# Changing over the two 64-token chunks of every second head pair in an RWKV recurrence

## The chip, the cores and the metric

The kernel runs on one core of a Trainium2 chip. The metric is the device time of one execution in microseconds, the median of several runs. All data are float32 in memory; the wide products are split into high and low float32r parts and take three passes each.

## The reference

One layer of a diffusion transformer: a feed-forward part, a mixer with two branches (retention and RWKV-7) in both directions over 1024 latent and 256 context tokens, and a second feed-forward part. The change concerns the RWKV branch, 8 heads of 64 in two directions:

```
def step(s, inp):                       # per token, per direction z and head
    rt, wt, kt, vt, at, bt = inp        # a = -kk, b = kk * a
    sa = einsum('zbhvk,zbhk->zbhv', s, at)
    s_new = s * wt[..., None, :] + sa[..., :, None] * bt[..., None, :] \
          + vt[..., :, None] * kt[..., None, :]
    y = where(is_fwd, einsum(s_new, rt), einsum(s, rt))
    return s_new, y
```

The output of both directions is added, normalised per head, scaled by `ln_w` and `ln_b`, a bonus term `sum(r * k * r_k) * v` is added, and the whole is multiplied by a gate.

## The kernel before

The stages follow each other: modulation vectors and the first feed-forward part (to about 1005 us of the trace), the projections of r, k, v and the low-rank decay terms (`rkv`, `lora_out`), then the recurrence, with the other projections of the mixer as filling work; then retention, the two output merges, the output projection and the second feed-forward part.

The 1280 tokens are cut into ten blocks of 128 (two of them context, p = 8 and 9), and each block into two chunks of 64. Both directions (z = 0 and 1) walk through the ten blocks, so there are 20 items, each of them for all 8 heads, kept as four head pairs `hp` with two heads `h` on the 128 partitions. For each item:

- `prep` (L738) loads the inputs, forms the decayed keys `bk` and queries `ar`, and multiplies them to the masked 128 x 128 matrices `g` (products `gps`, L793, copied by VectorE in L796). `ab(e)` gives the rows of chunk e: 64 to 127 for e = 0, 0 to 63 for e = 1.
- `inverse` (L828) inverts the 32 x 32 triangular blocks of `g` on VectorE, in 30 steps of two instructions (`invt` L846, `invx` L847), after a transfer through memory (`scr`, `invn`, L840) and a copy by ScalarE (L842) that spread the blocks over the partitions.
- `join` (L855) combines two 32-blocks to the inverse of 64: three sets of eight 32 x 32 products (`tps` L865, `hps` L868, `xps` L871) for e = 0, then the same for e = 1. Between the sets ScalarE copies (`tt`, L866 and L869), and VectorE writes the result back (L872). Each set has its own tile in PSUM, under the tag `us` with two buffers.
- `chain` (L874) is the recurrence: for each of the two chunks, the state products `q<-S,ar` (L888, four, 128 x 128 for latent blocks, which give the part for both halves of the partitions at once), the products of the chunk with v (`q<-wv,g`, L890, eight of 64 x 64), a copy `qa` (L892), the product with the inverse (`u<-qa,g`, L895, eight of 64 x 64), a copy to `wv` (L896), the state's addition (`u<-wv,bt`, L900, eight with 64 output rows, of which those of h = 0 and h = 1 lie in different halves), the state's decay on GpSimd (L902) and its sum on VectorE (L904), and for latent blocks the output products (`q<-wv,g`, L907, eight) and a copy or addition to `y` (L909, L911).
- `readout` normalises the finished blocks.

In one step all 24 products of L890, L895 and L907 have the same chunk e for all head pairs, so the same rows of the operands and the same rows of the output. There are 40 such steps, 32 of them with output.

`fill` runs beside it: `qkvg` and `gates` are 72 blocks of 24 wide products (`fps<-uh`, `fps<-ul`, L78 to L80, 512 or 256 columns), 1728 in all, whose weights are split by ScalarE (L67) and GpSimd (L68). The order of the instructions on each engine is not written out: a scheduler sets it from its own costs when the kernel is built, with the recurrence ahead of the fill by the order of the program.

The functions that the change touches, with what calls them:

Of the kernel before, what the change touches and what calls it, by code (L numbers as in the profile page):

```python
# [17 lines left out]
P = 128  # L18
# [377 lines left out]


class Mixer:
    def __init__(self, K, cst):
# [128 lines left out]
    def lora_out(self, c0, n, w2, pool, pk):  # L528
# [4 lines left out]
        def piece(q):  # L533
            if q == 0:
                st["x"] = pool.tile([96, 4, 512], F32R, tag="l2x", name="l2x", bufs=1)[:, :, :n]
                for b, s in enumerate("hlh"):
                    src = self.dram["wa" + s].rearrange("(q p) t -> p q t", p=32)[:, :, c0:c0 + n]
                    nc.sync.dma_start(out=st["x"][32 * b:32 * b + 32].bitcast(F32), in_=src)
            dst = self.dram[("td", "na")[q // 2] + str(q % 2)]
            for h0 in (0, 2):  # L540
                self.turns = self.turns[1:] + self.turns[:1]
                o = pool.tile([P, KT, P], F32, tag=self.turns[0], name="l2o", bufs=1).rearrange("p k c -> p (k c)").rearrange("p (h t) -> p h t", h=2)[:, :, :n]
                for j in range(2):
                    hp = h0 + j
                    ps = pk.tile([P, 512], F32, tag="l2", name="l2ps", bufs=2)[:, :n]
                    nc.tensor.matmul(ps, w2[:, q, hp * P:(hp + 1) * P], st["x"][:, q], start=True, stop=True)
                    nc.scalar.activation(o[:, j], ps, AF.Tanh, scale=0.5, bias=self.hw0[:, 4 * q + hp:4 * q + hp + 1])
                if q > 1:
                    nc.vector.tensor_scalar(out=o, in0=o, scalar1=-0.5, scalar2=-0.5, op0=ALU.mult, op1=ALU.add)
                nc.sync.dma_start(out=dst[h0:h0 + 2, :, c0:c0 + n].rearrange("h p t -> p h t"), in_=o)  # L550
        return [lambda q=q: piece(q) for q in range(4)]


    def rkv(self, u, pool, pp, pk):
# [8 lines left out]
        def heads(j, nm, hps):  # L563
# [14 lines left out]
            for hp, pad in zip(hps, pads):  # L578
                s = pool.tile([P, T], F32, tag="rs", name="rs", bufs=3)
                c = j * 4 + hp  # L580
                for t0, n in ((0, TL), (TL, TC))[:1 if j == 0 else 2]:
                    o = pcol(t0)
                    sv, pv = s[:, t0:t0 + n], pad[:, o:o + n]
                    nc.vector.tensor_tensor(out=sv, in0=pad[:, o - 1:o - 1 + n], in1=pad[:, o + 1:o + 1 + n], op=ALU.add)
                    nc.scalar.activation(pv, pv, AF.Copy, scale=om[:, c:c + 1])
                    nc.vector.scalar_tensor_tensor(out=sv, in0=sv, scalar=hm[:, c:c + 1], in1=pv, op0=ALU.mult, op1=ALU.add)
                    nc.sync.dma_start(out=self.dram[nm][hp, :, t0:t0 + n], in_=sv)
# [124 lines left out]
def ab(c):  # L712

    return 0 if c % 2 else 64

# [5 lines left out]
class Rwkv(Mixer):  # L721
# [16 lines left out]
    def prep(self, s, z, ring, tmp, pp):  # L738
# [62 lines left out]
        if z == 0 and lat:  # L801
# [4 lines left out]
            for hp in range(4):  # L806
                nc.tensor.matmul(ps[:, hp], self.cst["blk"], x[:, hp], start=True, stop=True)
            TT(out=x, in0=d["v"], in1=ps, op=ALU.mult)
            nc.sync.dma_start(out=self.dram["bv", p].rearrange("h p t -> p h t"), in_=x)
# [45 lines left out]
    def join(self, g, tmp, pq):  # L855

        nc, K = self.nc, self.K
        tt = tmp.tile([P, 8, 32], F32, tag="tt", name="tt")
        for e in range(2):
            of, os = ab(e), ab(e) + 32  # L860
            rf, rs = slice(of, of + 32), slice(os, os + 32)
            gb = lambda r, q, c: g[r, e, q // 2, q % 2, c]
            pst, psh, psx = (pq.tile([P, 8, 32], F32, tag="us", name=nm) for nm in ("tps", "hps", "xps"))
            for q in range(8):
                nc.tensor.matmul(pst[rf, q], gb(rf, q, rf), K.ident[rf, rf], start=True, stop=True, tile_position=(of, of))  # L865
            nc.scalar.activation(tt[rf], pst[rf], AF.Copy)  # L866
            for q in range(8):
                nc.tensor.matmul(psh[rs, q], gb(rf, q, rs), tt[rf, q], start=True, stop=True, tile_position=(of, os))  # L868
            nc.scalar.activation(tt[rs], psh[rs], AF.Copy)  # L869
            for q in range(8):  # L870
                nc.tensor.matmul(psx[rf, q], tt[rs, q], gb(rs, q, rs), start=True, stop=True, tile_position=(os, of))  # L871
            nc.vector.tensor_copy(out=g[rf, e, :, :, rs].rearrange("p a b t -> p (a b) t"), in_=psx[rf])  # L872

    def chain(self, un, z, y, first, last, tmp, ps_):  # L874
# [4 lines left out]
        hc = [slice(64 * h, 64 * h + 64) for h in range(2)]  # L879
        every = [(hp, h) for hp in range(4) for h in range(2)]  # L880
        lat, S = p < 8, self.S[z]
        f4 = lambda x: x.rearrange("p h v -> p (h v)")
        for e in (0, 1) if z == 0 else (1, 0):
            A, R = slice(ab(e), ab(e) + 64), slice(64 - ab(e), 128 - ab(e))
            q = ps_.tile([P, 4, P], F32, tag="q", name="q")
            qr, ac = (slice(0, P), slice(0, P)) if lat else (A, A)
            for hp in range(4):
                mm(q[qr, hp], ar[:, hp, e, ac], S[:, hp], start=hp == 0, stop=False)  # L888
            for hp, h in every:
                mm(q[A, hp, hc[h]], g[R, e, hp, h, A], wv[R, hp, e, hc[h]], start=False, stop=(hp, h) == (3, 1))  # L890
            qa = tmp.tile([P, 4, P], F32, tag="qa", name="qa")
            nc.scalar.activation(qa[A], q[A], AF.Copy)  # L892
            us = ps_.tile([P, 4, P], F32, tag="us", name="u")
            for hp, h in every:
                mm(us[A, hp, hc[h]], g[A, e, hp, h, A], qa[A, hp, hc[h]], start=True, stop=True)  # L895
            nc.scalar.activation(wv[A, :, e], us[A], AF.Copy)  # L896
            if not (last and e == 1 - z):
                st = us.rearrange("p h v -> p (h v)")[:, :256].rearrange("p (h v) -> p h v", h=4)
                for hp, h in every:
                    mm(st[hc[h], hp], bt[:, hp, e, hc[h]], wv[:, hp, e, hc[h]], start=True, stop=True)  # L900
                for h in range(2):
                    nc.gpsimd.tensor_tensor(out=S[hc[h], :, hc[h]], in0=S[hc[h], :, hc[h]], in1=pc[hc[h], e::2].unsqueeze(2).to_broadcast([64, 4, 64]), op=ALU.mult)  # L902
                for h in range(2):
                    nc.vector.tensor_tensor(out=S[hc[h], :, hc[h]], in0=S[hc[h], :, hc[h]], in1=st[hc[h]], op=ALU.add)  # L904
            if lat:
                for hp, h in every:
                    mm(q[R, hp, hc[h]], g[:, e, hp, h, R], wv[:, hp, e, hc[h]], start=False, stop=(hp, h) == (3, 1))  # L907
                if first:
                    nc.scalar.activation(y[R], f4(q[R]), AF.Copy)  # L909
                else:  # L910
                    nc.vector.tensor_tensor(out=y[R], in0=y[R], in1=f4(q[R]), op=ALU.add)  # L911
            yield

    def readout(self, p, y, tmp, pp):
# [20 lines left out]
        for hp in range(4):  # L935
            nc.vector.tensor_scalar(out=o[:, hp], in0=ps[:, hp], scalar1=K.vec["rwkv_ln_w"][:, hp:hp + 1], scalar2=K.vec["rwkv_ln_b"][:, hp:hp + 1], op0=ALU.mult, op1=ALU.add)
        x = y.rearrange("p (h t) -> p h t", h=4)
# [435 lines left out]
```

## Time and profile before

| | |
|---|---|
| median of three runs | 3313.97 us (3312.38 to 3322.35) |
| the profiled execution | 3323.0 us, span 3321.2 us |
| TensorE busy | 3093.0 us, 93% of the span |
| VectorE busy | 1893.6 us, 57% |
| ScalarE busy | 939.5 us, 28% |
| GpSimd busy | 819.1 us, 25% |
| mean granted TensorE clock | 0.939 |

Each line of the profile is a group of instructions of one line of the kernel, with the names of output and inputs, its form (partitions by elements; for products the part of the array that is used, rows by columns), its count, its busy time, the mean of one in nanoseconds, and the idle time ahead of it with what ended it. Products are pipelined, so the mean of one is longer than the distance to the next. Rows of waits give the total in us, the number and the longest.

### The profile page before, as it was taken

The numbers are of one execution on the slowest core, as the hardware profiler recorded it, in microseconds if no ns is written. First come the engines' busy times: TensorE is split into PE (matmuls) and PEld (weight loads), VectorE is DVE, ScalarE is ACT, GpSimd is POOL, SyncE is SP. The second block draws the span as 40 slices with busy tenths as digits, with TensorE's granted clock in tenths as the row PEclk, the third lists the DMA queues.
The fourth block names the chain that finished last, engine by engine and source line by source line (L and its number), as shares of the span: only waits on it lengthen the run. The fifth ranks groups of instructions, "written<-read, shape, count | busy, mean of one in ns | idle before, by whom it ended". The sixth has DMA issues, their size and how long they took to land.

```text
span 3321.2 us, 46574 instructions
## 1 busy us (share of the span) xinstructions
PE 3093.0 (93%) x18239; PEld 2577.0 (78%) x18239; DVE 1893.6 (57%) x3714; ACT 939.5 (28%) x1580; POOL 819.1 (25%) x628
## 2 busy tenths in 40 slices
PE   8999999999999997878888888888899999999998
PEld 4888888888887786667776776767778888888887
DVE  4876666444458855877775756764763432233226
ACT  5111111111125564333333334334322312111112
POOL 2111111111114214333333223332223212212210
PEclk9999999999999997878887887988999999999999
DMA  5432222111116356556444444444451112111211
GB/s 204 134 92 89 89 89 80 39 39 39 39 64 212 110 189 177 137 150 171 109 117 109 133 111 132 135 107 134 150 165 59 45 38 64 45 45 39 63 38 51
DMA packets 433540, 334.70 MB, mean 101 GB/s; under 512 B 87048, under 2 KB 365512, under 8 KB 433320
## 3 DMA queue, kind: packets, MB, share of 16 engines
q1 hardware_dynamic: 416768, 319.84, 32.4%
q10 hardware_dynamic: 16552, 11.90, 1.2%
q8 instruction: 143, 2.34, 0.3%
q14 instruction: 77, 0.63, 0.1%
HBM read 255.37 MB, written 72.09 MB: 99 GB/s over the span
## 4 chain that ended last, share of the span: by engine, by line
PE 66%; DVE 14%; DMA 11%; issue 3%; ACT 3%; SPq 2%; POOL 1%; DVEq 0%; ACTq 0%; POOLq 0%
PE psg L80 5%; PE psu L80 5%; PE psu L78 5%; PE psu L79 5%; PE psg L79 5%; PE psg L78 5%; PE psd L78 5%; PE psd L79 5%; PE psd L80 5%; DMA invn<-scr 5%; DVE invt L846 3%; DVE invx L847 3%; PE fps L78 1%; PE fps L80 1%; PE rps L79 1%
## 5 line engine op out<-in xcount | busy, mean ns | idle before, releaser
L68 POOL TENSOR_TENSOR wlo<-wraw,whi 128x1024 fp32r<-128x1024 f32 (+1 forms) x304 | 572.0, 1892 | 1862.4 <-ACT whi L67 1764.2
L260 DVE SCALAR_TENSOR_TENSOR h<-psd,g,h 128x512 f32<-128x512 f32 (+1 forms) x696 | 447.6, 670 | 466.8 <-PE psd L80 466.5
L67 ACT ACTIVATE whi<-wraw 128x1024 fp32r<-128x1024 f32 (+1 forms) x304 | 254.0, 853 | 498.9 <-PE psg L79 104.4
L78 PE MATMUL psd<-hh,whi 128*128 128x512 f32 (+1 forms) x912 | 333.3, 365 | 7.4 <-DVE h L260 7.3
L78 PE MATMUL psg<-uh,whi 128*128 128x512 f32 (+1 forms) x880 | 326.4, 371 | 3.7 <-ACT uh L132 3.2
L79 PE MATMUL psd<-hl,whi 128*128 128x512 f32 (+1 forms) x912 | 329.5, 361 | 0.0
L80 PE MATMUL psd<-hh,wlo 128*128 128x512 f32 (+1 forms) x912 | 329.0, 361 | 0.0
L79 PE MATMUL psg<-ul,whi 128*128 128x512 f32 (+1 forms) x880 | 326.6, 371 | 0.4 <-POOL ul L130 0.4
L80 PE MATMUL psg<-uh,wlo 128*128 128x512 f32 (+1 forms) x880 | 326.2, 371 | 0.0
L78 PE MATMUL psu<-uh,whi 128*128 128x512 f32 (+1 forms) x880 | 325.3, 370 | 0.3 <-ACT whi L67 0.3
L79 PE MATMUL psu<-ul,whi 128*128 128x512 f32 (+1 forms) x880 | 325.2, 370 | 0.0
L80 PE MATMUL psu<-uh,wlo 128*128 128x512 f32 (+1 forms) x880 | 325.0, 369 | 0.0
L78 PE MATMUL fps<-uh,whi 128*128 128x512 f32 (+1 forms) x576 | 247.3, 430 | 28.1 <-ACT whi L67 18.5
L245 DVE TENSOR_TENSOR sg<-sg,psu 128x512 f32<-128x512 f32 (+1 forms) x110 | 69.7, 633 | 313.7 <-PE psu L80 313.0
L80 PE MATMUL fps<-uh,wlo 128*128 128x512 f32 (+1 forms) x576 | 244.6, 425 | 2.4 <-POOL wlo L68 2.3
L79 PE MATMUL fps<-ul,whi 128*128 128x512 f32 (+1 forms) x576 | 243.6, 423 | 0.0
L846 DVE TENSOR_TENSOR invt<-invx,invn 128x60 f32<-128x60 f32 (+5 forms) x600 | 202.4, 340 | 65.2 <-issue 28.9
L247 ACT ACTIVATE hh<-sg 128x512 fp32r<-128x512 f32 (+1 forms) x110 | 64.7, 588 | 570.5 <-DVE sg L245 493.4
L847 DVE TENSOR_TENSOR invx<-invx,invt 128x60 f32<-128x60 f32 (+5 forms) x600 | 196.0, 329 | 29.3 <-issue 8.0
L78 PEld LDWEIGHTS psd<-hh,whi 128*128 128x128 f32 x912 | 172.0, 189 | 38.7 <-DVE h L260 12.2
L244 ACT ACTIVATE sg<-psg 128x512 f32<-128x512 f32 (+1 forms) x110 | 60.4, 550 | 474.3 <-PE psg L80 474.2
L80 PEld LDWEIGHTS psd<-hh,wlo 128*128 128x128 f32 x912 | 171.9, 189 | 26.7
(323 smaller groups left out, 5709.5 us busy)
## 6 DMA issues: line engine op xcount, KB each, us to landing
wraw<-in_w_in_dram SPq DMA_DIRECT2D x144, 256.0 KB
modw<-in_w_mod_dram SPq DMA_DIRECT2D x112, 256.0 KB
wraw<-in_ffn_w_gate_dram SPq DMA_DIRECT2D x44, 512.0 KB
wraw<-in_ffn_w_up_dram SPq DMA_DIRECT2D x44, 512.0 KB
wraw<-in_ffn_w_down_dram SPq DMA_DIRECT2D x44, 512.0 KB
invn<-scr SPq DMA_DIRECT2D x20, 512.0 KB
modw<-in_w_mod_dram SPq DMA_DIRECT2D x16, 512.0 KB
wraw<-in_w_in_dram SPq DMA_DIRECT2D x12, 512.0 KB
```

Source lines behind the costliest of these rows:

```text
L67: nc.scalar.activation(hi[:, s], raw, AF.Copy)
L68: nc.gpsimd.tensor_tensor(out=lo[:, s], in0=raw, in1=hi[:, s].bitcast(F32), op=ALU.subtract)
L78: mm(ps, w[0][:, ws], x[0][xs], start=start, stop=False)
L79: mm(ps, w[0][:, ws], x[1][xs], start=False, stop=False)
L80: mm(ps, w[1][:, ws], x[0][xs], start=False, stop=stop)
L244: nc.scalar.activation(s, psg, AF.Silu)
L245: nc.vector.tensor_tensor(out=s, in0=s, in1=psu, op=ALU.mult)
L247: nc.scalar.activation(hh, s, AF.Copy)
L260: nc.vector.scalar_tensor_tensor(out=hs, in0=ps, scalar=gates()[v][:, m:m + 1], in1=hs, op0=ALU.mult, op1=ALU.add)
L846: eng.tensor_tensor(out=tv, in0=x[:, :m, i:i + 1].to_broadcast([P, m, w]), in1=n[:, i:i + 1, i + 1:].to_broadcast([P, m, w]), op=ALU.mult)
L847: eng.tensor_tensor(out=x[:, :m, i + 1:], in0=x[:, :m, i + 1:], in1=tv, op=ALU.add)
```

## The change

In the arrays r, k, v, kk, td and na that the projection stage leaves in memory, the two chunks of every block are changed over for the odd head pairs (hp = 1 and 3). A step that handles chunk e then takes slot `c[hp] = e ^ (hp & 1)`, so that odd pairs work on the other half of the partitions. The loops over the head pairs are written so that neighbours alternate (`other`). Further edits follow from it:

- The state products become half as wide in output rows (64), four for the half that is needed first and, for latent blocks, four more for the other half after the u products (L918 after).
- Each copy of qa, wv and y becomes two, one for the even and one for the odd pairs.
- `join` takes both chunks together, alternating between them: three sets of sixteen products and three PSUM tiles, where six of eight had been.
- The bonus is multiplied by v in four instructions, one for each head pair, where it was one; `readout` reads the turned columns; in `rkv` the odd pairs' last instruction is split in two.

```
+def turned(x, hp):
+    x = x.rearrange("p (b c t) -> p b c t", c=2, t=64)
+    return x[:, :, ::-1] if hp % 2 else x
...
-                    nc.scalar.activation(o[:, j], ps, AF.Tanh, scale=0.5, bias=self.hw0[:, 4 * q + hp:4 * q + hp + 1])
+                    nc.scalar.activation(turned(o[:, j], hp), turned(ps, 0), AF.Tanh, scale=0.5, bias=self.hw0[:, 4 * q + hp:4 * q + hp + 1])
...
+                    s4 = turned(sv, 0)
+                    nc.vector.tensor_tensor(out=s4, in0=turned(pad[:, o - 1:o - 1 + n], hp), in1=turned(pad[:, o + 1:o + 1 + n], hp), op=ALU.add)
...
+                    p4 = turned(pv, hp)
+                    for x, y in [(sv, pv)] if hp % 2 == 0 else [(s4[:, :, i], p4[:, :, i]) for i in range(2)]:
+                        nc.vector.scalar_tensor_tensor(out=x, in0=x, scalar=hm[:, c:c + 1], in1=y, op0=ALU.mult, op1=ALU.add)
...
-            TT(out=x, in0=d["v"], in1=ps, op=ALU.mult)
+            for hp in range(4):
+                TT(out=turned(x[:, hp], hp), in0=turned(d["v"][:, hp], 0), in1=turned(ps[:, hp], 0), op=ALU.mult)
...
-        for e in range(2):
-            for q in range(8):
-                nc.tensor.matmul(pst[rf, q], gb(rf, q, rf), K.ident[rf, rf], start=True, stop=True, tile_position=(of, of))
-            nc.scalar.activation(tt[rf], pst[rf], AF.Copy)
+        for q in range(8):
+            for e, of, os, rf, rs in ers:
+                nc.tensor.matmul(pst[rf, q], gb(e, rf, q, rf), K.ident[rf, rf], start=True, stop=True, tile_position=(of, of))
+        for e, of, os, rf, rs in ers:
+            nc.scalar.activation(tt[rf], pst[rf], AF.Copy)
...
-            A, R = slice(ab(e), ab(e) + 64), slice(64 - ab(e), 128 - ab(e))
+            c = [e ^ (hp & 1) for hp in range(4)]
+            A, R = [slice(ab(x), ab(x) + 64) for x in c], [slice(64 - ab(x), 128 - ab(x)) for x in c]
             for hp in range(4):
-                mm(q[qr, hp], ar[:, hp, e, ac], S[:, hp], start=hp == 0, stop=False)
-            for hp, h in every:
-                mm(q[A, hp, hc[h]], g[R, e, hp, h, A], wv[R, hp, e, hc[h]], start=False, stop=(hp, h) == (3, 1))
+                mm(q[A[hp], hp], ar[:, hp, c[hp], A[hp]], S[:, hp], start=hp < 2, stop=False)
+            for hp, h in other:
+                mm(q[A[hp], hp, hc[h]], g[R[hp], c[hp], hp, h, A[hp]], wv[R[hp], hp, c[hp], hc[h]], start=False, stop=hp > 1 and h == 1)
-            nc.scalar.activation(qa[A], q[A], AF.Copy)
+            for i in range(2):
+                nc.scalar.activation(qa[A[i], i::2], q[A[i], i::2], AF.Copy)
...
+            if lat:
+                for hp in range(4):
+                    mm(q[R[hp], hp], ar[:, hp, c[hp], R[hp]], S[:, hp], start=hp < 2, stop=False)
-            nc.scalar.activation(wv[A, :, e], us[A], AF.Copy)
+            for i in range(2):
+                nc.scalar.activation(wv[A[i], i::2, c[i]], us[A[i], i::2], AF.Copy)
...
-                if first:
-                    nc.scalar.activation(y[R], f4(q[R]), AF.Copy)
-                else:
-                    nc.vector.tensor_tensor(out=y[R], in0=y[R], in1=f4(q[R]), op=ALU.add)
+                y4 = y.rearrange("p (h v) -> p h v", h=4)
+                for i in range(2):
+                    yo, qo = y4[R[i], i::2], q[R[i], i::2]
+                    if first:
+                        nc.scalar.activation(yo, qo, AF.Copy)
+                    else:
+                        nc.vector.tensor_tensor(out=yo, in0=yo, in1=qo, op=ALU.add)
```

The scheduler gives all engines a new order. TensorE in the middle of the recurrence, before: the end of a join (xps), u products of both directions, then their state and output products (names are output and inputs, then stationary columns by moving columns, then the count in a row):

```order
L871 MATMUL xps<-g,tt 32x32 x8
L895 MATMUL u<-qa,g 64x64 x8
L817 MATMUL btps<-ident,bk 128x128 x8
L895 MATMUL u<-qa,g 64x64 x8
L900 MATMUL u<-wv,bt 64x64 x8
L907 MATMUL q<-wv,g 64x64 x8
L822 MATMUL vtps<-ident,in_v 128x128 x4
L900 MATMUL u<-wv,bt 64x64 x8
L907 MATMUL q<-wv,g 64x64 x8
L888 MATMUL q<-S_10080,ar 128x128 x4
L890 MATMUL q<-wv,g 64x64 x8
```

The same place in a comparable step of the changed kernel (L915 is u, L918 the second set of state products, L876 and L882 the join's first and second set, L924 the state's addition, L933 the output products):

```order
L915 MATMUL u<-qa,g 64x64
L876 MATMUL tps<-ident,g 32x32 x2
L915 MATMUL u<-qa,g 64x64 x7
L918 MATMUL q<-S_10090,ar 64x128 x4
L876 MATMUL tps<-ident,g 32x32 x14
L933 MATMUL q<-wv,g 64x64
L918 MATMUL q<-S_10091,ar 64x128 x4
L79 MATMUL fps<-ul,whi 128x512
L924 MATMUL u<-wv,bt 64x64 x8
L933 MATMUL q<-wv,g 64x64 x7
L882 MATMUL hps<-tt,g 32x32 x16
```

The second set of state products, of half width, stands behind u, and the join's sets are of sixteen.

TensorE at the end of the fill, before: the last fill product stands ahead of the last four groups of u products, with a join and the recurrence's other products behind it.

```order
L80 MATMUL fps<-uh,wlo 128x512
L865 MATMUL tps<-ident,g 32x32 x8
L900 MATMUL u<-wv,bt 64x64 x8
L907 MATMUL q<-wv,g 64x64 x8
L868 MATMUL hps<-tt,g 32x32 x8
L888 MATMUL q<-S_10081,ar 128x128 x4
L890 MATMUL q<-wv,g 64x64 x8
```

The changed kernel at the last u products of the recurrence:

```order
L80 MATMUL fps<-uh,wlo 128x512
L915 MATMUL u<-qa,g 64x64 x8
L918 MATMUL q<-S_10091,ar 64x128 x4
L80 MATMUL fps<-uh,wlo 128x512
L962 MATMUL ytps<-ident,y 128x128 x4
L78 MATMUL fps<-uh,whi 128x512
L79 MATMUL fps<-ul,whi 128x512
```

Here fill products stand on both sides of the last u products. Of the 1728 fill products 301 stood ahead of the end of the first group of u products, 1427 between it and the end of the last, and none behind; now these are 275, 1143 and 310. The 310 are followed by the products of the RWKV merge (`rwps`) and by retention, whose first products stood between the last groups of u before.

More of the change, by code (lines that the diff above doesn't have):

```diff
@@ L899, in chain @@
                 for hp, h in every:
[L900 to L904, printed above, removed]
-            if lat:
-                for hp, h in every:
-                    mm(q[R, hp, hc[h]], g[:, e, hp, h, R], wv[:, hp, e, hc[h]], start=False, stop=(hp, h) == (3, 1))
-                if first:
-                    nc.scalar.activation(y[R], f4(q[R]), AF.Copy)
-                else:
-                    nc.vector.tensor_tensor(out=y[R], in0=y[R], in1=f4(q[R]), op=ALU.add)
+                    mm(st[hc[h], hp], bt[:, hp, c[hp], hc[h]], wv[:, hp, c[hp], hc[h]], start=True, stop=True)
+                p4 = pc.rearrange("p (a x) -> p a x", x=4)
+                p4 = (p4[:, :, 0::3] if e == 0 else p4[:, :, 1:3]).unsqueeze(3).to_broadcast([P, 2, 2, 64])
+                for r in hc:
+                    nc.gpsimd.tensor_tensor(out=four(S[r, :, r]), in0=four(S[r, :, r]), in1=p4[r], op=ALU.mult)
+                for r in hc:
+                    nc.vector.tensor_tensor(out=S[r, :, r], in0=S[r, :, r], in1=st[r], op=ALU.add)
+            if lat:
+                for hp, h in other:
+                    mm(q[R[hp], hp, hc[h]], g[:, c[hp], hp, h, R[hp]], wv[:, hp, c[hp], hc[h]], start=False, stop=hp > 1 and h == 1)
+                y4 = y.rearrange("p (h v) -> p h v", h=4)
[5 more added lines that the diff above has]
+                        nc.vector.tensor_tensor(out=yo, in0=yo, in1=qo, op=ALU.add)
             yield
@@ L935, in readout @@
         for hp in range(4):
-            nc.vector.tensor_scalar(out=o[:, hp], in0=ps[:, hp], scalar1=K.vec["rwkv_ln_w"][:, hp:hp + 1], scalar2=K.vec["rwkv_ln_b"][:, hp:hp + 1], op0=ALU.mult, op1=ALU.add)
+            nc.vector.tensor_scalar(out=turned(o[:, hp], 0), in0=turned(ps[:, hp], hp), scalar1=K.vec["rwkv_ln_w"][:, hp:hp + 1], scalar2=K.vec["rwkv_ln_b"][:, hp:hp + 1], op0=ALU.mult, op1=ALU.add)
         x = y.rearrange("p (h t) -> p h t", h=4)
```

32 lines of the change are left out of this document (17 added, 15 removed).

## The prediction

> **What bounds the kernel now.** I began with the page's granted clock (40 slices of 83 us) and then cut the span into stages.
>
> ```profile
> PEclk9999999999999997878887887988999999999999
> ```
>
> The clock is short of full only from slice 16 to slice 28. There lies the recurrence with its fill products, and every instruction of the change that repeats.
>
> ```profile
> core 0: us, PE busy (x) PEld busy (x) DVE busy (x) ACT busy (x) POOL busy (x), PEclk, DMA share, GB/s
> 1310.00:2262.00 952.00, 807.97 (x6779) 672.38 (x6777) 657.14 (x1754) 335.17 (x646) 310.95 (x308) 0.84 0.47 126
> 2262.00:2310.00 48.00, 38.34 (x447) 35.58 (x447) 23.10 (x69) 22.64 (x47) 7.71 (x7) 0.82 0.50 156
> 2310.00:2475.00 165.00, 147.88 (x827) 125.43 (x826) 117.85 (x305) 53.40 (x87) 40.39 (x21) 0.94 0.49 151
> 2475.00:2650.00 175.00, 169.13 (x743) 138.65 (x743) 70.05 (x93) 54.48 (x77) 54.44 (x26) 0.98 0.24 72
> ```
>
> In the 952 us TensorE is busy for 808 us at a clock of 0.84. At full clock that is about 808 x 0.84 = 679 us of work, so 273 us are lost to waiting and to the low clock. The boundaries are events, from the views of two products:
>
> ```profile
> L895 PE MATMUL u<-qa,g x640: 218/218/367, 1397.1 to 2308.8; 64*64 64x64 f32 x160
> L80 PE MATMUL fps<-uh,wlo x576: 274/389/797, 1261.6 to 2261.7; 128*128 128x512 f32 x171, 128*128 128x256 f32 x21
> ```
>
> The last fill product starts at 2262, the last u product of the recurrence at 2309; what follows up to 2475 is retention and the two output merges. Next the chain of work from 1310 to 2310, and the waits there:
>
> ```profile
> by line: DMA invn<-scr 15.9%; DVE invt L846 9.7%; DVE invx L847 8.8%; issue 7.5%; PE fps L78 3.7%; PE fps L80 3.6%; PE fps L79 3.5%; PE gps L793 3.0%; ACT invx L842 2.2%; DMA wraw<-in_w_in_dram 2.1%; DMA scr<-invx 2.0%; DMA scr<-g 2.0%; PE
> ```
> ```profile
> DVE invx L850 <- ACT invx L842: 60.5, 9, 8.9
> DVE g L872 <- PE xps L871: 38.7, 12, 7.2
> PE hps L868 <- ACT tt L866: 19.3, 5, 6.2
> ```
>
> The triangular inverse (its transfer and its VectorE steps) has 34% of the chain, the fill 11%, and the small products come after that. No engine is full: TensorE, VectorE and the inverse's transfer wait for each other in fixed orders. So work taken off TensorE is worth something between its whole length and what it has on the chain.
>
> **The change part by part.** First the pace of small products; a float32 product leaves two records, so 16 are one group of eight.
>
> ```profile
> 1530.81 1.14 PE L890 MATMUL q<-wv,g 64*64 64x64 f32 x16
> 1533.38 1.14 PE L895 MATMUL u<-qa,g 64*64 64x64 f32 x16
> 1534.45 0.69 PE L865 MATMUL tps<-ident,g 32*32 32x32 f32 x16
> 1535.06 1.16 PE L793 MATMUL gps<-ar,bk 64*128 64x128 f32 x16
> 1537.30 0.69 PE L900 MATMUL u<-wv,bt 128*64 128x64 f32 x16
> ```
> ```profile
> 1966.28 0.19 PE L865 MATMUL tps<-ident,g 32*32 32x32 f32 x1
> 1966.28 0.19 PE L871 MATMUL xps<-g,tt 32*32 32x32 f32 x1
> 1966.31 0.19 PE L865 MATMUL tps<-ident,g 32*32 32x32 f32 x1
> 1966.32 0.19 PE L871 MATMUL xps<-g,tt 32*32 32x32 f32 x1
> ```
>
> L890 and L895 keep all eight products on one quarter of the array and take 1.14 us. L900 alternates between column halves and takes 0.69. The change makes L890, L895 and L907 alternate: 40 + 40 + 32 groups at 0.45 us less, 50 us. The second set shows 32-row products of two quarters starting in pairs, two in 0.03 us, where one quarter needs 0.03 each. The join's 120 groups of eight become 60 of sixteen at about the old 0.69 us: 60 x 0.5 = 30 us (lower end 0, as no whole group of the kind is there). The state products (L888) become two sets of half width where there is an output. A pair of alternating 128-wide products costs what one costs, by L793 (16 in 1.16 us; L888 has 8 in about 1.09), so I take 0; unpaired they would add 0.9 x 32 = 29 us, and in the eight steps without an output pairing may save 3. Together -80 us at full clock, ends -21 and -83.
>
> The Trainium skill, "TensorE: Matmul & The Clock Gate", Part 3, says that a weight load overlaps products in flight only when the row group differs. L900 differs in columns only and still runs at 0.69, so the row decides; by that rule L907, also of full rows, would gain nothing, and the 80 would be 66.
>
> What is added, with its rows:
>
> ```profile
> L892 ACT ACTIVATE qa<-q 64x512 f32<-64x512 f32 x40 | 23.7, 592 | 36.9 <-PE q L890 36.4
> L866 ACT ACTIVATE tt<-tps 32x256 f32<-32x256 f32 x40 | 14.7, 367 | 19.7 <-PE tps L865 19.1
> L902 POOL TENSOR_TENSOR S<-S,pc 64x256 f32<-64x256 f32 x72 | 49.9, 694 | 57.3 <-PE q L888 49.1 <-DVE invt L846 2.2 <-DVE invx L847 1.7
> L904 DVE TENSOR_TENSOR S<-S,u 64x256 f32<-64x256 f32 x76 | 31.6, 416 | 16.9 <-PE u L900 15.4
> L911 DVE TENSOR_TENSOR y<-y,q 64x512 f32<-64x512 f32 x14 | 9.6, 684 | 4.9 <-DMA y<-d_y 4.7
> L808 DVE TENSOR_TENSOR in_r<-in_v,bops 128x512 f32<-128x512 f32 x8 | 5.5, 688 | 10.0 <-PE bops L807 9.9
> L804 DVE SCALAR_TENSOR_TENSOR in_r<-m,vec,in_r 128x128 f32<-128x128 f32 x32 | 12.6, 439 | 0.0
> ```
>
> - Each copy of qa, wv and of the first y becomes two of half length. A half has 256 elements as L866 has, so 2 x 367 against 592: +0.14 us, 96 times, 14 us (ends 0 and 57, if a half costs as much as a whole). Of these 80 stand between products of the recurrence.
> - y's additions: 2 x 416 - 684 = +0.15 us x 16. bv: 4 x 439 - 688 = +1.1 us x 8. Together 11 us of VectorE, bounded below by 0.
> - The decay of S on POOL now waits for the second state set, which stands behind the u products. It takes 2 x 0.69 = 1.39 us, beside the copies of wv (0.73) and L900 (0.69), 1.42 us in all. So it is hidden, narrowly; with late semaphores it may add 0.3 x 32 = 10 us. Queued behind it on POOL are weight splits, which have slack (POOL is busy 311 of 952 us).
> - The layout turns in the projection stage cost TensorE nothing and VectorE ten additional half-length instructions; they lie beside TensorE work (235 of 245 us):
>
> ```profile
> 1005.00:1250.00 245.00, 235.12 (x1134) 192.06 (x1132) 177.62 (x212) 140.62 (x215) 67.33 (x96) 0.99 0.49 170
> ```
>
> I put +12 us of all this on the recurrence's path, ends 0 and 40.
>
> Then the moved work. By the order, 1427 fill products stood between the first and the last u, and now 1143; after the last u there were none, and now there are 310. In the stage after 2475 wide products pass at 175/743 = 0.235 us, so the 310 cost 73 us, with nothing beside them but the last readouts. What does taking 284 out of the recurrence give? Four rounds of it (four u groups each; fill products alone, count in brackets) show that:
>
> ```profile
> 1662.20:1754.90 92.70, 41.28 (x142) 30.02 (x142) 1.37 (x2) 3.55 (x6) 0.87 0.44 116
> 1754.90:1852.20 97.30, 31.75 (x109) 23.34 (x109) 0.67 (x1) 2.98 (x5) 0.79 0.45 113
> 1944.00:2040.00 96.00, 39.12 (x139) 27.25 (x139) 0.00 (x0) 3.57 (x6) 0.86 0.42 109
> 2040.00:2156.20 116.20, 58.38 (x210) 42.89 (x210) 0.00 (x0) 4.69 (x8) 0.87 0.54 152
> ```
>
> From the third to the fourth a product costs (116.2 - 96.0)/71 = 0.285 us; from the second to the third 30 more cost nothing. I take 0.2 (-57 us), nearer the first pair, which differs by more products; ends 0 and -81.
>
> **The sum**, made at the end of the fill (2262), by two readings.
> - TensorE's: the lost 273 us stay whole, the work is 80 us less, and the last four steps, which ran after the fill (38 us at 0.82), now run inside it, about +20: -60.
> - The chain's: the last u comes earlier by 57, and by half of the small saving (80/0.84 = 95, so 47), less 12: at 2309 - 92 = 2217; plus 73 the fill ends at 2290: +28.
>
> The middle is -16. After the fill 213 us went by up to 2475, 48 of them shared with the recurrence's end; the same 20 us leave that stretch, with a little waiting: -22. Sum -38. The profiled execution took 3323.0 us (span 3321.2), so 3285; it lies 9 us above the median of three, 3314, which gives 3276.
>
> **The rivals.**
> - TensorE's reading holds more than fully: lost time shrinks with the work, 952 x 619/679 = 868, -84 - 22 = -106, at 3208; with the loss whole, -82. For it: the longest of the four rounds is the one with most fill. Against: the inverse's share of the chain.
> - Slower. The inverse paces the recurrence, and the fill that was free inside it is now exposed behind it. A fill product is worth 0.1 (-28), a third of the small saving arrives (-30), costs are 15: last u at 2266, fill end 2339, +77 - 22 = +55, at 3369. It decides where the last u falls: the fill must end by 2262 + 22, so the last u must be 98 us earlier, by 2211. For it: VectorE waits 60 us for the copy that follows the inverse's transfer, which no product shortens. Against: it also waits 39 us for the join's products.
> - No change. With less fill TensorE waits longer, and the clock falls towards the 0.79 of the second round above. At 0.80 the 619 us left there take 619/0.80 - 619/0.84 = 37 us more, which eats the 38. The Trainium skill, "TensorE: Matmul & The Clock Gate", Part 1, says that about 3.4 us of idleness return TensorE to half rate; the 0.84 of the first stage agrees.
> - The pairs don't overlap. L890, L895 and the join will write one bank from two row groups at a time, and no row here shows that case; the L865 and L871 pairs write two tiles. If such a bank takes one at a time, 14 us (L907) of the 80 are left: by TensorE's reading +6, by the chain's -57 - 8 + 12 + 73 + 2309 - 2262 = +67, in the middle +36, less 22: +14, at 3328. The Trainium skill, "TensorEngine Tiling (Array Packing)", Gotcha 1, says that different row tiles can't access one bank together.
>
> **How the numbers follow.** Forecast (-70 to -12) 0.42; TensorE's rival 0.22; no change 0.12; slower 0.16; pairs without overlap 0.08. About 0.3%, 10 us, is what can be told from no change. So faster 0.64, same 0.12, slower 0.24. The range runs from 3214 (-100) to 3335 (+21), which leaves out the far half of the slow rival and the end of the fast one; the forecast's own is 3244 to 3302.
>
> **What would show it.** L890, L895 and L907 at about 0.69 us a group, their busy time nearly halved; the join in three groups of sixteen at about 0.7; the last u near 2217, the last fill product near 2246 (the sum's -16); the clock between 1310 and 2262 not under 0.84; fewer VectorE waits on xps. It is wrong if the groups stay at 1.1 us, or if the last u comes after 2211 by more than the later stretch wins back.

## The result and the profile after

The changed kernel is slower: 3352.01 us, the median of four runs (3343.81 to 3356.99), where the kernel before took 3314.63 on the same chip. The ratio is 1.0106, with a 95% interval of 1.0076 to 1.0136. The predicted time was 3276, and the range ended at 3335. All ratios below are to the kernel before, run beside each kernel on the same chip; the chip differs between groups of runs, and the kernel before took 3315 to 3320 us there, so differences of a few us across groups mean little.

The profiled execution took 3343.81 us, with a span of 3342.0. It is the shortest of its four, and the profiled one of before (3323.0) is longer than all that were timed there (3312 to 3322), so the two traces differ by 21 us where the medians differ by 37; only the 21 can be followed in them. Ahead of 1310 us and behind the start of the output projection little differs: from the first product `ops` to the end of the span it is 845 us before and 842 after. Nearly all of the difference lies between. The products `u` and the fill, from the views of two products (first and last start):

```profile
L915 PE MATMUL u<-qa,g x640: 217/218/367, 1400.3 to 2248.4; 64*64 64x64 f32 x160
L80 PE MATMUL fps<-uh,wlo x576: 277/389/796, 1260.8 to 2329.7; 128*128 128x512 f32 x171, 128*128 128x256 f32 x21
```

The recurrence ends 60 us earlier than before (2248 against 2309), the fill 68 us later (2330 against 2262). The stages cut at these events, and the granted clock of the page:

```profile
core 0: us, PE busy (x) PEld busy (x) DVE busy (x) ACT busy (x) POOL busy (x), PEclk, DMA share, GB/s
1310.00:2248.00 938.00, 701.95 (x7052) 555.08 (x7054) 642.17 (x1833) 335.69 (x718) 296.27 (x290) 0.80 0.46 121
2248.00:2330.00 82.00, 76.68 (x365) 62.55 (x366) 20.78 (x32) 33.21 (x55) 43.12 (x31) 0.98 0.64 194
2330.00:2500.00 170.00, 154.30 (x890) 133.53 (x889) 108.93 (x305) 58.75 (x104) 29.65 (x15) 0.95 0.43 139
```
```profile
PEclk8999999999999997777678888799999999999999
```

To the end of the fill TensorE's work at full clock is 702 x 0.80 + 76.7 x 0.98 = 637 us. The stretch is 1020 us long, so 383 us are lost to waiting and to the low clock, where 273 were lost before up to the end of the fill (290 up to 2310, with the last four steps counted in). Up to the end of the fill TensorE has 42 us less to do, and 110 us more are lost: the end comes 68 us later. The second row is the exposed part: 82 us of almost nothing but fill, with VectorE busy for 21.

The small products themselves do what was forecast. First a group of sixteen records (eight products) of L907 before, then from the changed kernel one of L933 (L907 before), L909 (L890 before) and L915 (L895 before), four of the state products (L907, half as wide now) and fifteen of the sixteen products of a set of the join (L888, L882):

```profile
1623.60 1.10 PE L907 MATMUL q<-wv,g 128*64 128x64 f32 x16
```
```profile
2238.77 0.69 PE L933 MATMUL q<-wv,g 128*64 128x64 f32 x16
1535.26 0.69 PE L888 MATMUL xps<-g,tt 32*32 32x32 f32 x30
1535.87 0.68 PE L915 MATMUL u<-qa,g 64*64 64x64 f32 x16
1545.21 0.66 PE L907 MATMUL q<-S,ar 128*64 128x128 f32 x8
1545.80 0.68 PE L909 MATMUL q<-wv,g 64*64 64x64 f32 x16
1527.71 0.69 PE L882 MATMUL hps<-tt,g 32*32 32x32 f32 x30
```

The 1.14 us of L890 and L895 have become 0.68, and the 1.10 of L907 0.69. That is the pace of groups that nothing interrupts; in the whole stretch, where other products stand between them and the clock is lower, the busy time of L890 and L895 fell by a third (58.5 to 38.1 us and 51.3 to 35.0), not by nearly half, and that of L907 hardly (36.7 to 35.0). The waits between 1310 and 2330:

```profile
ACT invx L854 <- DMA invn<-scr: 131.0, 13, 13.8
POOL S L928 <- PE q L918: 79.8, 18, 12.8
DVE invx L862 <- ACT invx L854: 62.6, 8, 15.2
DVE g L890 <- PE xps L888: 26.2, 5, 19.5
```

VectorE waits for the copy that follows the inverse's transfer as long as before (62.6 us; 60.5 before), and less for the join (26.2; 38.7 before). GpSimd waits 80 us for the second set of state products, where it waited 49 for the one set of before.

Where the fill stands is seen in its products alone, by rounds of four u groups (steps 5 to 8, 9 to 12, 13 to 16, 17 to 20, then the last round, steps 37 to 40, and what stands behind it):

```profile
1452.90:1536.30 83.40, 32.19 (x118) 24.70 (x118) 0.68 (x1) 2.39 (x5) 0.75 0.53 136
1536.30:1626.40 90.10, 14.24 (x81) 11.62 (x81) 0.00 (x0) 1.12 (x3) 0.72 0.42 99
1626.40:1700.10 73.70, 4.74 (x27) 3.88 (x27) 0.00 (x0) 0.36 (x1) 0.62 0.32 78
1700.10:1788.60 88.50, 29.39 (x98) 18.17 (x98) 0.00 (x0) 2.52 (x5) 0.82 0.58 157
2163.20:2248.40 85.20, 65.54 (x245) 47.41 (x245) 0.00 (x0) 5.93 (x10) 0.94 0.55 170
2248.40:2330.00 81.60, 73.22 (x310) 58.69 (x310) 0.00 (x0) 7.60 (x13) 0.98 0.64 194
```

Two rounds, steps 9 to 16, hold 81 and 27 products, and the clock falls to 0.72 and 0.62. They take 164 us all the same. The 310 products at the end cost 82 us.

### The profile page after: what moved, and what is told of

The parts are those of the page before. It is cut to its first block, busy times and chain, and to the rows that moved or that the text cites. A ratio compares the mean times of both kernels' runs of the same rounds, so it can differ in the third digit from the quotient of the medians.

```text
span 3342.0 us, 47251 instructions
## 1 busy us (share of the span) xinstructions
PE 3027.6 (91%) x18495; PEld 2492.1 (75%) x18495; DVE 1865.4 (56%) x3764; ACT 956.4 (29%) x1677; POOL 828.3 (25%) x628
## 4 chain that ended last, share of the span: by engine, by line
PE 66%; DVE 16%; DMA 10%; issue 4%; ACT 3%; SPq 1%; POOL 0%; DVEq 0%; ACTq 0%; POOLq 0%
PE psg L80 5%; PE psu L78 5%; PE psu L79 5%; PE psg L78 5%; PE psu L80 5%; PE psg L79 5%; PE psd L78 5%; PE psd L79 5%; PE psd L80 5%; DVE invt L858 3%; DVE invx L859 3%; DMA invn<-scr 3%; PE fps L80 1%; PE fps L78 1%; PE fps L79 1%
## 5 line engine op out<-in xcount | busy, mean ns | idle before, releaser
L858 DVE TENSOR_TENSOR invt<-invx,invn 128x60 f32<-128x60 f32 (+9 forms) x600 | 190.4, 323 | 53.8 <-issue 22.6
L859 DVE TENSOR_TENSOR invx<-invx,invt 128x60 f32<-128x60 f32 (+9 forms) x600 | 182.6, 309 | 52.0 <-DMA in_v<-d_v 11.5
L79 PEld LDWEIGHTS psd<-hl,whi 128*128 128x128 f32 x912 | 172.3, 189 | 26.6
```

Source lines behind the costliest of these rows:

```text
L79: mm(ps, w[0][:, ws], x[1][xs], start=False, stop=False)
L858: eng.tensor_tensor(out=tv, in0=x[:, :m, i:i + 1].to_broadcast([P, m, w]), in1=n[:, i:i + 1, i + 1:].to_broadcast([P, m, w]), op=ALU.mult)
L859: eng.tensor_tensor(out=x[:, :m, i + 1:], in0=x[:, :m, i + 1:], in1=tv, op=ALU.add)
```

## The experiments

Three theories stood at the start: the scheduler's order (fill left behind the recurrence), the inverse that paces the recurrence, and the waits that the change adds. In all tables a round is four u groups; its fill products are counted from the records.

### The two halves, the fill's order, and the wait on GpSimd

`e1_join_only` is the kernel before with the new `join` alone; `e2_turn_only` the changed kernel with the old `join`. `e3_fill_ahead` has the changed kernel's instructions and gives the scheduler a priority for each fill block, counted from the start of the recurrence:

```
+    def pace(self):
+        want = self.p0 + 0 + 85 * self.nb
+        self.nb += 1
+        return self.tc.high_priority(offset=max(0, self.tc.cur_priority - want))
...
+                    with self.pace():
+                        ps = self.block(u, n, 512 * i + hd * P, pp)
```

`e4_free_decay` writes the decayed state to a tile of its own, so that GpSimd need not wait for the second set of state products:

```
-                    nc.gpsimd.tensor_tensor(out=four(S[r, :, r]), in0=four(S[r, :, r]), in1=p4[r], op=ALU.mult)
+                    nc.gpsimd.tensor_tensor(out=four(sd[r]), in0=four(S[r, :, r]), in1=p4[r], op=ALU.mult)
...
-                    nc.vector.tensor_tensor(out=S[r, :, r], in0=S[r, :, r], in1=st[r], op=ALU.add)
+                    nc.vector.tensor_tensor(out=S[r, :, r], in0=sd[r], in1=st[r], op=ALU.add)
```

> The kernel before with the edit of the join alone (three sets of sixteen products, two chunks alternating); no chunk is changed over. In its order 172 fill products stand behind the last u product. Theory 'order' (the time went into fill products that the scheduler moved behind a recurrence which VectorE and the inverse pace): 172 x 0.235 = 40 us exposed, 20 to 35 won in the recurrence, so 3315 to 3340 us. Rival 'added waits' (the second set of state products, the halved copies and GpSimd's later decay of S slow the recurrence): none of them is in this kernel, so 3285 to 3315.

> The changed kernel with the join of before. Its order has no fill product behind the last u product, and 1431 between the first and the last, as before has 1427. 'Order': what the overlapping products win stays, 3280 to 3312 us. 'Added waits': all of them are in, 3335 to 3360 us.

> The changed kernel with nothing edited but the scheduler's priority of the fill: block k of 72 gets the priority of the start of the recurrence plus 85 k, so that none of the 1728 fill products stands behind the last u product (1712 ahead of the 37th group of u, as before had). 'Order': 3270 to 3315 us, at least 30 below the changed kernel. 'Added waits': the waits are all still there, 3335 us or more.

> The changed kernel with GpSimd's decay of S written to a tile of its own, so that it no longer waits for the second set of state products; 311 fill products behind the last u product, as in the changed kernel (310). 'Order': no change against the changed kernel, 3340 to 3360 us. 'Added waits': the wait of GpSimd (80 us on L918 in the changed kernel's profile) is gone, 3300 to 3330 us.

| kernel | median us | ratio to before | last u | last fill | behind the last u |
|---|---|---|---|---|---|
| e1_join_only | 3297.67 | 0.9942 (0.9924 to 0.9959) | 2237.4 | 2286.6 | 172 |
| e2_turn_only | 3305.5 | 0.9962 (0.9945 to 0.9978) | 2286.0 | 2264.2 | 0 |
| e3_fill_ahead | 3290.87 | 0.9909 (0.9877 to 0.9941) | 2293.4 | 2239.8 | 0 |
| e4_free_decay | 3346.07 | 1.0083 (1.0054 to 1.0112) | 2244.5 | 2329.2 | 311 |

Each half alone is faster than before, and both together are slower, which speaks against a loss in either half's instructions. (Each of these kernels has an order of its own, though, and the later runs show how much hangs on that.) e3 has the same instructions as the changed kernel and is 61 us faster, so the order costs it that much against this one. In its profile the fill ends 90 us earlier:

```profile
L923 PE MATMUL u<-qa,g x640: 218/218/367, 1396.8 to 2293.4; 64*64 64x64 f32 x160
L80 PE MATMUL fps<-uh,wlo x576: 278/389/795, 1267.4 to 2239.8; 128*128 128x512 f32 x171, 128*128 128x256 f32 x21
```

In e4 GpSimd no longer waits for L918 (its decay now waits for the state's sum), and the time stays. That speaks against the added wait as the cause. It doesn't exclude it, as this kernel's order is another too: its first four middle rounds (steps 5 to 20) hold 80, 40, 122 and 149 products where the changed kernel has 118, 81, 27 and 98.

```profile
POOL sd L929 <- DVE S L931: 173.6, 34, 19.1
```

The run of the join alone was a miss for the order theory: with 172 products behind it was expected at 3315 us or more, and it came where the theory of the added waits had put it.

### Controls, and the recurrence with no fill

`c1_before_ahead` and `c2_join_ahead` put e3's priorities on the kernel before and on the join alone. `x1_before_alone` and `x2_after_alone` make room in SBUF scarce, by a tile that is used once, so that the fill's tiles can't be had until the recurrence is over; all but 48 products then stand behind it:

```
+        self.room = keep.tile([P, 1024], F32, tag="room", name="room")
+        nc.vector.memset(self.room, 0.0)
+        nc.vector.tensor_copy(out=self.S[0][:, 0, 64:128], in_=self.room[:, 0:64])
```

> The kernel before with the same priority of the fill as in the fill-ahead kernel, and no edit of the change. Theory 'the change wins, its order loses': before's own order has its fill ahead already (1715 of 1728 by the 36th group of u), so the priority gives it nothing, 3308 to 3328 us, some 25 above the fill-ahead kernel (3291). Rival 'the priority wins': 3280 to 3300 us, and the change itself is worth nothing.

> The join's edit alone, with the fill ahead by the same priorities. 'Order': the join alone with its own order (172 fill products behind) took 3298 us; with none behind 3280 to 3297, and the chunk turn adds little to it. Rival 'the turn carries the gain of the fill-ahead kernel': no better than 3298, 3298 to 3312.

> The kernel before with 4 KB a partition more held by the recurrence, so that the fill finds no room beside it: 48 of 1728 fill products stand ahead of the first u group, none among the others. It shows the length of the recurrence (first to last u product) by itself. 'The inverse and VectorE pace it': 780 to 880 us, little under before's 912 with all fill in it. Rival 'TensorE paces it': 912 less 304 us of fill, 600 to 680 us.

> The changed kernel in the same way. 'The inverse and VectorE pace it': its recurrence alone is 0 to 50 us shorter than before's alone, and within 60 us of the 848 that it took with 1143 fill products inside. Rival 'TensorE paces it': 80 to 110 us shorter than before's alone.

c1 took 3322.33 us, 1.0005 (0.9987 to 1.0024); c2 3320.16, 1.0004 (0.9988 to 1.0021). So the priorities give the kernel before nothing. c2 was a miss of the order theory, and lies above its rival's range too: it has none behind and lost the 0.6% that the join alone had won.

x1 and x2, one run each, took 3611.68 and 3582.34 us. Between the first and the last u lie 752 us (1376.2 to 2127.8) and 726 us (1374.0 to 2100.3): 26 us are all that the change gives to the recurrence when nothing stands beside it, by one execution of each. The 752 lie between the two ranges that had been named for x1 (780 to 880, and 600 to 680), so they bear out neither theory. The 26 are within the range of the inverse's theory; the 726 are not, as they are 122 under the changed kernel's 848 where 60 had been allowed. The eight middle rounds (steps 5 to 36), of x1 and then of x2:

```profile
1441.00:2083.60 642.60, 444.12 (x4495) 400.73 (x4493) 418.99 (x1380) 174.93 (x350) 108.67 (x139) 0.59 0.29 68
```
```profile
1420.00:2061.90 641.90, 371.74 (x4736) 308.92 (x4734) 419.27 (x1429) 194.74 (x445) 105.46 (x140) 0.61 0.30 71
```

TensorE is busy for 72 us less, and the stretch is as long as before: 80.3 and 80.2 us a round. VectorE has the same 419 us in both. So all but 1 of the 26 us lie in the first four and the last four steps, and the rounds between give nothing.

### How many products stand behind

`c3_turn_ahead` completes the table of halves (the turn alone, with e3's priorities). `d1`, `d2` and `d3` are the changed kernel with other numbers in `want`:

```
-        want = self.p0 + 0 + 85 * self.nb
+        want = self.p0 + 0 + 105 * self.nb      d1
+        want = self.p0 + 300 + 125 * self.nb    d2
+        want = self.p0 + 0 + 70 * self.nb       d3
```

> Only the turn of the chunks, the join as before, and the same priorities of the fill as in e3 and the two controls. The turn alone left no fill product behind the last u already (3305 us), and with the priorities none is behind either. 'The fill left behind is the loss': nothing to win back, 3295 to 3315. 'Any other order moves the time, whatever is behind': it may fall outside, as the join's control did with +22 us: 3320 to 3330, or 3275 to 3290.

> The changed kernel with priorities of the fill that leave 189 products behind the last u, between e3 (none, 3291) and the changed kernel (310, 3352). 'The fill left behind is the loss': 61 us over 310 products is 0.2 us each, so 3291 + 37 = 3328 (3315 to 3340). 'The changed kernel's loss is one bad stretch of its own order (steps 11 to 14, where no fill stands)': this order has fill in all steps, so 3285 to 3310.

> The changed kernel with later priorities of the fill: 256 products behind the last u. 'The fill left behind is the loss': 3291 + 50 = 3341 (3328 to 3355), and slower than the run with 189. 'One bad stretch': 3285 to 3315, and no order between the two.

> The changed kernel with earlier priorities of the fill: all 1728 products stand ahead of the 31st of 40 u groups, so ten groups run with no fill at all. 'The fill left behind is the loss': none is behind, 3285 to 3300 as in e3. 'What counts is that fill stands in every group': the last ten groups run at the pace without fill (18 us each, TensorE half idle) and the other thirty at a higher price for each product (0.29 us, as between two rounds of the kernel before): 3305 to 3335.

c3 took 3297.94 us, 0.994 (0.9916 to 0.9964). d1 took 3315.57 us, 0.9999 (0.9981 to 1.0017); d2, with more products behind, 3308.95, 0.9981 (0.9969 to 0.9993); d3, with none behind, 3329.77, 1.004 (1.0024 to 1.0057). c3 came within what the theory of the products behind had named, and d1 at the lower edge of it. With d2 and d3 that theory falls: d2 should have been slower than d1, and d3 as fast as e3. The bad stretch of the changed kernel's own order was borne out by d2 and missed by d1; d3 came where the rival that wants fill in every group had put it. The turn alone beats the kernel before in both of its orders (e2 and c3, 0.9962 and 0.994), the join alone in one of two (e1 and c2); two orders are too few to say more. In d2 the two rounds that the changed kernel leaves with 81 and 27 products hold 102 and 138:

```profile
1544.10:1617.60 73.50, 23.07 (x102) 18.18 (x102) 0.00 (x0) 1.90 (x5) 0.65 0.63 164
1617.60:1723.30 105.70, 44.32 (x138) 27.93 (x138) 0.69 (x1) 2.96 (x5) 0.84 0.45 116
```

By step 36 d2 has done 1310 products at 2157 us, the changed kernel 1173 at 2163. Of these 137 fewer, 132 are missing from the two rounds, and they are done at the end, at about 0.25 us each (81.6 us for 310 is 0.26): 33 of the 39 us by which d2's output projection starts earlier (2461 against 2500).

### The inverse left out, and the hole filled

`y1` and `y2` are x1 and x2 with a larger room tile, so that no fill at all stands ahead of the last u, and without the call of `inverse`:

```
-            self.inverse(un[i]["g"], nc.vector, tmp)
```

`r1` and `r2` give priorities to a few fill blocks alone:

```
+        want = self.p0 + 0 + 100 * self.nb if 20 <= self.nb < 28 else self.tc.cur_priority    r1
+        want = self.p0 + 0 + 85 * self.nb if 21 <= self.nb < 30 else self.tc.cur_priority     r2
```

> The kernel before without fill beside the recurrence (as in x1) and also without the inverse of the 32 x 32 blocks, with its transfers (the products then use the blocks as they are). With the inverse a round of four u groups took 80 us on the mean and the recurrence 752 us from the first to the last u. 'The inverse paces the round': the rounds fall to 60 us or less, the recurrence to under 600. 'The recurrence's own products, copies and sums pace it': 72 to 80 us a round, 680 to 752.

> The same of the changed kernel: no fill beside the recurrence and no inverse. With the inverse it took 726 us, its rounds 80 us as before the change. 'The inverse paces the round and hides what the change saves': without it the changed kernel is shorter than the kernel before by more than the 26 us with it, 40 to 95 us. 'The change saves little on the path anyway': again 0 to 30 us.

> The changed kernel with earlier priorities for eight fill blocks alone (the 21st to the 28th), which then stand in steps 9 to 16; all others keep theirs, and 272 products are left behind the last u (310 in the changed kernel, 256 in d2). 'A round has room for about 100 products, and two rounds were left with 81 and 27': 90 products of room by 0.29 us are 26 us, with the 30 us or so of hole, 3310 to 3328. 'What is behind costs 0.2 us each': 3344 (3336 to 3352).

> The same for nine blocks (the 22nd to the 30th) with a smaller distance between them: the hole is filled, and 160 products are behind. 'Room in the rounds': all rounds hold 95 or more, so no better than r1: 3303 to 3325, as d1 and d2. 'What is behind costs 0.2 us each': 3322, 22 us less than r1.

y1 and y2, one run each, took 3369.54 and 3268.25 us, a difference of 101. The recurrence takes 566 us (1309.2 to 1875.4) and 461 (1307.8 to 1768.9), 105 less. The eight middle rounds:

```profile
1363.50:1831.70 468.20, 422.89 (x4547) 383.11 (x4546) 219.84 (x378) 156.69 (x304) 112.56 (x143) 0.64 0.23 67
```
```profile
1352.10:1733.20 381.10, 323.92 (x4786) 269.80 (x4784) 216.99 (x411) 172.41 (x391) 112.71 (x140) 0.75 0.29 84
```

That is 58.5 us a round before and 47.6 after, where both took 80 with the inverse. The 58.5 and the 566 are what the inverse's theory had named; the 105 lie a little above its 40 to 95. So the inverse (its transfers, its copy and its 60 VectorE instructions, left out together) paces the round, and with it in place 79 of the 105 us that the change saves don't show. Which of its parts does it wasn't tried, nor whether it is the inverse's chain or VectorE's load as a whole, which falls from 419 us to 220. And the 105 are not all TensorE's work: in these rounds it falls, as busy time by clock, only from 271 us (422.9 at 0.64) to 243 (323.9 at 0.75), 28 us, which would be 44 at 0.64. Of the 99 us by which its busy time falls, the other 55 are by this estimate the higher clock.

r1 took 3333.4 us, 1.0046 (1.003 to 1.0063), and r2 3330.64, 1.0029 (1.0013 to 1.0046). Filling the hole won 19 us with 272 products still behind, a third of the 61; with 160 behind it won 21. The price of 0.2 us for each product behind would have given r1 8 us; the room theory wanted 24 to 42. r1 lies between the two ranges and r2 outside both, so neither theory prices the order.

### Two more orders

The changed kernel again, with other numbers: `g1` with `600 + 85` (28 products in the third round, none behind), `g2` with `-300 + 85` (no hole, none behind).

> The changed kernel with priorities of the fill that leave nothing behind the last u but only 28 products in the third round (steps 13 to 16); the last round takes 240. 'Room in the rounds': 77 products of room lost by 0.29 us are 22 us above e3, 3313 (3303 to 3325). 'What stands behind is the loss': as e3, 3285 to 3298.

> The changed kernel with priorities that leave nothing behind and no round but the last under 117 products. Both 'room in the rounds' and 'what stands behind': 3285 to 3300, as e3. 'Orders with the same amounts differ by chance', as d2 and r1 did by 24 us: it may as well be 3300 to 3325, and e3's 3291 is partly a lucky order.

g1 took 3329.21 us, 1.0028 (1.0012 to 1.0044), and g2 3329.64, 1.0025 (1.0006 to 1.0044). Both miss what either theory named for them; g2 is nearest to the third case, chance in the order, and 5 us above its range too. All nine orders of the changed kernel's same instructions:

| order | behind | fill in the eight middle rounds | ratio to before |
|---|---|---|---|
| the changed kernel's own | 310 | 118 81 27 98 112 123 174 115 | 1.0106 |
| e3 | 0 | 147 108 121 165 186 152 283 130 | 0.9909 |
| d1 | 189 | 120 136 132 117 90 132 170 122 | 0.9999 |
| d2 | 256 | 121 102 138 71 116 157 141 109 | 0.9981 |
| d3 | 0 | 142 142 209 254 169 249 192 0 | 1.0040 |
| r1 | 272 | 95 149 115 98 94 147 107 179 | 1.0046 |
| r2 | 160 | 95 146 135 183 152 99 139 146 | 1.0029 |
| g1 | 0 | 122 95 28 152 166 186 236 148 | 1.0028 |
| g2 | 0 | 160 155 125 165 146 211 246 117 | 1.0025 |

Their mean is 1.0018, and they lie between 0.9909 and 1.0106. The kernel before stood at 1 and 1.0005 in two orders. The changed kernel's own order is the worst of its nine and e3 the best, the only one that beats the kernel before by more than 0.3%; seven of nine lie within 0.5% of before. The orders were chosen, not drawn, so the mean is a hint; but e3 against the kernel before, taken alone, would have shown a gain of 0.9% that the other orders don't bear out.

What the rounds have in common: over the 80 middle rounds of the changed kernel's runs (these nine orders, and x2 without fill), one takes 83 us with no fill (9 rounds), 77 with 1 to 90 products (5), 82 with 90 to 120 (19), 89 with 120 to 150 (23), 103 with 150 to 200 (17) and 123 with more (7). By these means up to about 100 products a round lengthen it by nothing, and a further one costs about 0.3 us, with 10 us of scatter for one round. Eight of the nine rounds with no fill are those of x2, at a clock of 0.61, so the flat part may in part be a balance: less fill, but slower small products. That wasn't tried apart. One product behind the last u costs about as much (0.26) as one too many in a round, so by these two prices moving it wins little, and what an order can lose is room that it leaves unused. r1 and g2 show that this isn't all.

## Why the prediction was wrong

- **The small products** had the pace that was forecast, and a little less of the gain. Groups went from 1.14 to 0.68 us, forecast at 0.69. TensorE's work to the end of the fill and the recurrence fell from the prediction's 679 + 20 = 699 us at full clock to 637, 62 less where 80 were taken. (The last 48 us before hold 38 x 0.82 = 31 us of work, of which about 12 are retention's first products.) The split state products are a part of the difference: 72 sets at 0.66 against 40 at 1.09 are +4 us, where 0 was taken. L907, whose products use all rows, gained in pace too (1.10 to 0.69), so the 80 need not shrink to 66 on its account; but its busy time hardly fell, with only 5 of its 32 groups uninterrupted.
- **Pairs in one bank** do overlap: the eight products of L909 go to one tile `q` from two row groups, in 0.68 us. That rival is refuted. Neighbours lie on different halves of the output rows as well, so this is the case of two quarters, not of two row groups alone. The Trainium skill, "TensorEngine Tiling (Array Packing)", Gotcha 1, says that different row tiles can't access one bank together; in this trace they write one tile in turn, at 0.68 us where one row group took 1.14, and the measurement decides. Whether two of them are ever in the bank at the same instant is not shown.
- **TensorE's reading** is the step that failed first. It let the lost 273 us stay whole. They grew to 383: with no fill beside it the round stays at 80 us although TensorE has less to do (x1 and x2), so work taken off TensorE becomes waiting, and fill taken out of the rounds comes back behind them. The reading gave -60 at the end of the fill, and +68 was measured; the forecast's 2246, the middle of both readings, came at 2330. Averaging a reading that says "TensorE's work sets the time" with one that says "the chain sets it" had no ground; the chain of waits, with 34% in the inverse, had said which.
- **The chain's reading** gave +28. Its price of what is left behind was near (73 us; 82 measured). Its last u at 2217 was 31 us early: half of the small saving (47) was to arrive, and alone 26 arrive; 284 products taken out of the recurrence were to bring 57, but they came in part out of rounds that had room for them. The price of 0.2 came from four of the eight rounds of before; another, with 163 products in 72.6 us (1487.8 to 1560.4), fits no price.
- **The slower rival** has the mechanism: the inverse paces the recurrence, and the fill that was free inside it is exposed behind. It put the last u at 2266 and the fill's end at 2339 (2248 and 2330 measured), and the last u by 2211 that it asked of a gain didn't come. It had 0.16. That its fill's end is only 9 us off is partly luck: its last u is 18 us late, and what is behind was priced 9 us too low. Its third of the small saving, 30 us, is near the 26 that x1 and x2 show, but those lie at the two ends of the recurrence.
- **The added waits** were put at +12 us. No run shows the 0.3 us a step by which late semaphores were to delay GpSimd's decay; with that wait taken out (e4) the time stayed.
- **The tail** after the fill shrank by more than the 22 us taken, from 214 (2261.7 to 2475.7) to 171 (2329.7 to 2500.4); the recurrence's end no longer lies in it. So +68 - 43 - 4 (behind 2500) make the +21 us of the profiled executions.
- **The clock** was to stay at 0.84 or above between 1310 and 2262 and fell to 0.80, the value that the "no change" rival named.
- **What the prediction didn't hold at all** is how much hangs on the order. It priced the moved fill by the piece, while the same work in nine orders spans 2%, by more than the pieces explain. Filling the hole won back 19 of the 37 us of the changed kernel's own order (r1). What makes up the rest of it, and why e3 is 40 us faster than g2, with none behind in both and over 100 products in each of their eight middle rounds, stays open.

## What to carry to other kernels

Where a serial chain on another engine paces a loop, less work on TensorE is worth only what it shortens with that chain in place: run the loop without its filler, with the chain and without it, before the saving is priced. Filling work cost this loop nothing up to a certain amount a round and 0.3 us a product beyond it, so look where the scheduler put it, round by round, and not only at how much is left behind. Before a change of 1% is believed in a kernel whose order a scheduler sets, run the same instructions in several orders.

## What had not been expected of the hardware

With no fill beside it the recurrence runs at a granted clock of 0.59 to 0.61 (the rows of x1 and x2), and the same product of `u` takes 311 ns in the median where it took 218 beside the fill:

```profile
L918 PE MATMUL u<-qa,g x640: 218/311/366, 1374.0 to 2100.3; 64*64 64x64 f32 x160
```

So beside the fill the small products have the higher clock (0.80 to 0.84). How much of the time TensorE is busy doesn't tell the clock by itself: with neither fill nor inverse y1 is busy for 90% of its rounds at 0.64, and y2 for 85% at 0.75. x2's rounds, at 0.61 and 311 ns, take 80 us, about as long as those with up to 100 fill products. Whether they would be shorter at the higher clock isn't shown.
